# One accumulator for both parts of x, operands at multiples of 512 bytes, and moved steps in a hybrid decoder layer

## The chip, the cores and the metric

The kernel runs on one core of a Trainium2 chip. TensorE multiplies, VectorE, ScalarE and GpSimd work on elements, SyncE issues the transfers; each of them works through its own queue strictly in order. In the profile they are called PE (its weight loads PEld), DVE, ACT, POOL and SP. The metric is the device time of one execution in microseconds (us), the median of the runs; less is better.

## What is computed

One decoder layer on 256 tokens of width 1024, in float32. It has three parts, each followed by a residual and a layer norm:

```python
def swiglu(x, w_gate, w_up, w_down):
    return (jax.nn.silu(x @ w_gate) * (x @ w_up)) @ w_down
...
h = layer_norm(DEEPNORM_ALPHA * h + 0.5 * swiglu(h, ffn1_w_gate, ffn1_w_up, ffn1_w_down), ln1_g, ln1_b)
h = layer_norm(DEEPNORM_ALPHA * h + hybrid_mixer(h, w_in, ...), ln2_g, ln2_b)
h = layer_norm(DEEPNORM_ALPHA * h + 0.5 * swiglu(h, ffn2_w_gate, ffn2_w_up, ffn2_w_down), ln3_g, ln3_b)
```

Both SwiGLU blocks have 2816 inner columns. The mixer projects h with `w_in` into z, xBC (4096 columns), dt, q, k, v and two gates. xBC goes through a causal depthwise convolution of four taps and SiLU, then through a chunked scan (Mamba-2 SSD) of 8 groups; q, k and v go through causal attention of 8 heads; both branches are projected, gated, added and projected once more.

## The kernel before

**Products in three parts.** Every float32 operand is held as a pair of float32r tiles, hi (the rounded value) and lo (what is left). A product is hi·hi + lo·hi + hi·lo, accumulated in PSUM. `xT` holds x transposed, as [128, 8 k-tiles, 2 parts, 256 tokens], so the two parts of a k-tile lie side by side.

**The weight stream.** 126 weight tiles of 1 MB (2048 columns a partition) run through three buffers each of `raw`, `hi` and `lo`. A tile is prepared in two pieces of 1024 columns: ACT casts `hi<-raw` (line 91), and DVE, for some pieces POOL, subtracts `lo<-raw,hi` (line 100). `step()` moves a counter on by one before every batch of products; it runs what tables have due at this count, prepares the next pieces (hi four ahead, lo three ahead, or up to a number given as `upto`), and runs what was put behind them. `at`, `later`, `after` and `at_mid` fill these tables, so the order on each engine is written by hand. A step of a token-major product is 12 matmuls of 512 columns (`mm3`: four hi·hi, four lo·hi, then what is due "mid", then four hi·lo).

**Weights-stationary products** (`fmm`, `wstat`) have 128 weight columns standing still and x moving. For each of four k-tiles there is one matmul of 512 columns, both parts of x at once (line 274), and then one of 256 columns for lo of the weights (line 276). A call therefore makes 8 matmuls; the left half of the accumulator holds the sum for x hi, the right half that for x lo, and the product is their sum. In the kernel 240 such calls run: 72 in each SwiGLU, 64 for xBC, 32 for q and k. Who takes a product copies the right half with ACT into `fb` and adds the left half with DVE one step later: `gate` (line 392) and `h` (400) in SwiGLU, `pre` (598) ahead of the convolution, `qk` (148 is the line that runs tabled calls). The convolution of a 128-column block is then one ACT multiplication and three DVE multiply-adds on `pre` and `cv`, both in SBUF (line 608). PSUM has eight banks: four for `mmt` tiles, four for `smt` tiles.

**The order around the boundaries.** After the first SwiGLU come the layer norm, 16 steps of z, 32 of xBC, 16 of q and k. The decay `dt` goes through a long chain of small POOL and DVE operations, which ends in `da` (line 564); `acum_mm` (569 to 575) multiplies it by a triangular matrix in step 15 of the mixer, between two batches of z. The scan groups start after xBC and are spread over the steps of q, k, v and the gates. At the end of the mixer eight steps of the output projection `wo` run, four for the first 128 tokens, four for the others; after each half comes `ln`, and `to_T` transposes the normalised tokens again into `xT` (lines 242 to 246) in the middle of a later step. Then the second SwiGLU starts with `gu`, x standing still.

**Places in SBUF.** Constant tiles are laid out in the order in which they are made, each rounded up to 32 bytes. `tok`, `ident` and `tri` start 128 bytes past a multiple of 512, `xT` 192 bytes past one; the weight tiles, `hTh` and `hTl` start at multiples of 512.

Of the kernel before, what the change touches and what calls it, by code (L numbers as in the profile page):

```python
# [15 lines left out]
P = 128  # L16
# [23 lines left out]
def tile_decoder_layer(ctx: ExitStack, tc: tile.TileContext,  # L40
# [18 lines left out]
    # ---------------------------------------------------------------- weight stream  # L59
    # Every tile holds 2048 columns a partition, in two pieces of 1024: raw from DRAM, then hi + lo in float32r.  # L60
# [72 lines left out]
    def after(d, fn, *a):  # L133
        """As later, but behind the pieces of that step."""
        at_after(clk["n"] + d, fn, *a)

    def step(i, h, upto=None):
        """The next products, on tile i: what is due, then the pieces to come."""
# [3 lines left out]
        if upto is not None:  # L142
            stream(2 * i + upto, 2 * i + upto)
# [6 lines left out]
    def first_order(tiles, n=3):  # L150
        """Both token blocks of every tile; t = 1 of the first n tiles comes after their t = 0."""
# [21 lines left out]
    # ---------------------------------------------------------------- the order of the weights  # L173
# [34 lines left out]
    s_f2 = ffn_specs(f2g, f2u, f2d, [(), (1,), (0, 1), ()])  # L208

    # ---------------------------------------------------------------- constants and inputs  # L210
# [25 lines left out]
    xT = const.tile([P, KD, 2, S], F32R, name="xT")  # L236
# [23 lines left out]
    def xmm(ps, k0, t, i):  # L260
        """ps (tokens of t, 512) += x k-tiles k0.. times the weight tile i: x stands still."""
# [699 lines left out]
```

## Time and profile before

| | |
|---|---|
| median of 3 runs | 799.17 us (798.56 to 799.29) |
| span of the profiled execution | 794.7 us |
| time of a run beyond that span | about 4.5 us |
| PE, DVE, ACT, POOL busy | 97%, 70%, 55%, 18% |
| matmuls, and weight loads | 4042, and as many |
| moved by DMA | 143.61 MB, mean 181 GB/s |
| granted TensorE clock, mean | 0.990 |

The span goes from the first to the last instruction of the profiled execution. A run's time also holds what lies around it, so a sum made on the span has 4.5 us added before it is set beside the median. PE's busy time is modelled: a matmul is recorded with its full latency, and the next one starts before it has ended. What a matmul costs in a dense run is the distance between the starts of two of them, not its duration.

### The profile page before, as it was taken

How to read it: one execution, taken by the hardware profiler on the slowest of the kernel's cores; microseconds unless marked ns; L12 is line 12 of the kernel's file. 1: busy time of each engine (PE TensorE's matmuls, PEld its weight loads, DVE VectorE, ACT ScalarE, POOL GpSimd, SP SyncE). 2: the span in 40 equal slices, each digit the busy share in tenths (PEclk: the TensorE clock that was granted, in tenths of full speed). 3: DMA queues.
4: the chain of work that ended last, by engine and by line, in shares of the span. 5: the costliest groups of instructions: out<-in, count | busy, mean ns of one | idle time of the engine just before them, and what ended most of it. 6: DMA issues, size and time to landing. Idle time of an engine off the chain costs nothing.

```text
span 794.7 us, 10749 instructions
## 1 busy us (share of the span) xinstructions
PE 767.6 (97%) x4042; PEld 651.4 (82%) x4042; DVE 556.2 (70%) x817; ACT 438.7 (55%) x766; POOL 142.8 (18%) x217
## 2 busy tenths in 40 slices
PE   7999999999999999998999999999998999999996
PEld 6888888888777888777888878888887888888885
DVE  4676667448533999998877786776686677667446
ACT  5565556333554666678666663575553555656420
POOL 1000000004042222202866764000012000000000
PEclk9999999999998999999999999999999999999998
DMA  8666665673544454467555534444564576556611
GB/s 317 219 215 220 202 212 169 206 261 106 165 159 160 154 165 159 159 212 232 166 186 185 159 123 172 159 157 134 182 214 158 189 235 212 178 193 212 210 55 54
DMA packets 68356, 143.61 MB, mean 181 GB/s; under 512 B 3968, under 2 KB 8528, under 8 KB 68304
## 3 DMA queue, kind: packets, MB, share of 16 engines
q1 hardware_dynamic: 68160, 142.79, 54.1%
q8 instruction: 32, 0.52, 0.3%
q14 instruction: 20, 0.16, 0.1%
q10 hardware_dynamic: 144, 0.13, 0.0%
HBM read 141.83 MB, written 1.08 MB: 180 GB/s over the span
## 4 chain that ended last, share of the span: by engine, by line
PE 51%; DVE 14%; issue 5%; POOL 3%; ACT 3%; DVEq 0%; ACTq 0%; POOLq 0%
PE w L274 12%; PE w L276 6%; DVE cv L608 6%; DVE lo L100 5%; PE b L252 5%; PE b L258 5%; PE b L254 5%; PE dn L252 2%; PE dn L254 2%; PE dn L258 2%; PE yp L692 2%; ACT hi L91 1%; PE gu L254 1%; PE gu L258 1%; DVE pre L598 1%
## 5 line engine op out<-in xcount | busy, mean ns | idle before, releaser
L100 DVE TENSOR_TENSOR lo<-raw,hi 128x1024 fp32r<-128x1024 f32 x235 | 295.4, 1272 | 96.1 <-ACT hi L91 95.0
L91 ACT CAST hi<-raw 128x1024 fp32r<-128x1024 f32 x252 | 259.2, 1046 | 95.7 <-issue 37.6
L274 PE MATMUL w<-xT,hi 128*128 128x512 f32 x960 | 262.4, 396 | 4.4 <-DVE qk L148 3.0
L274 PEld LDWEIGHTS w<-xT,hi 128*128 128x128 f32 x960 | 163.2, 188 | 26.9 <-DVE qk L148 3.4
L276 PEld LDWEIGHTS w<-xT,lo 128*128 128x128 f32 x960 | 145.3, 188 | 25.4 <-DVE lo L100 4.2
L276 PE MATMUL w<-xT,lo 128*128 128x256 f32 x960 | 149.6, 278 | 3.3 <-DVE lo L100 3.2
L100 POOL TENSOR_TENSOR lo<-raw,hi 128x1024 fp32r<-128x1024 f32 x17 | 43.7, 2584 | 354.3 <-DVE lo L100 187.2
L608 DVE SCALAR_TENSOR_TENSOR cv<-pre,vecs,cv 128x255 f32<-128x255 f32 (+2 forms) x96 | 63.6, 666 | 2.4
L387 ACT COPY fb<-w 128x256 f32<-128x256 f32 x72 | 26.8, 373 | 54.5 <-PE w L276 53.6
L258 PE MATMUL dn<-lo,hTh 128*128 128x512 f32 (+1 forms) x176 | 47.9, 377 | 0.0
L254 PE MATMUL dn<-hi,hTl 128*128 128x512 f32 (+1 forms) x176 | 47.8, 377 | 0.0
L252 PE MATMUL dn<-hi,hTh 128*128 128x512 f32 (+1 forms) x176 | 47.8, 377 | 0.0
L254 PEld LDWEIGHTS dn<-hi,hTl 128*128 128x128 f32 x176 | 32.3, 188 | 6.2
L258 PEld LDWEIGHTS dn<-lo,hTh 128*128 128x128 f32 x176 | 32.2, 188 | 5.9
L252 PEld LDWEIGHTS dn<-hi,hTh 128*128 128x128 f32 x176 | 31.7, 188 | 5.7
L343 POOL TENSOR_TENSOR tok<-tok,lng 128x256 f32<-128x256 f32 x1 | 0.9, 872 | 187.9 <-ACT tok L340 187.9
L614 ACT ACTIVATE g<-cv 128x256 f32<-128x256 f32 x32 | 13.3, 416 | 33.5 <-DVE cv L608 33.1
L320 ACT ACTIVATE lnmv<-lnmv,epsc 128x1 f32<-128x1 f32 x6 | 1.8, 296 | 52.2 <-DVE lnmv L319 52.2
L252 PE MATMUL b<-hi,xT 128*128 128x512 f32 x96 | 27.6, 409 | 0.0
L258 PE MATMUL b<-lo,xT 128*128 128x512 f32 x96 | 25.9, 392 | 0.0
L254 PE MATMUL b<-hi,xT 128*128 128x512 f32 x96 | 25.8, 391 | 0.0
L254 PEld LDWEIGHTS b<-hi,xT 128*128 128x128 f32 x96 | 18.0, 188 | 4.0
(209 smaller groups left out, 1063.4 us busy)
## 6 DMA issues: line engine op xcount, KB each, us to landing
raw<-in_w_in_dram SPq DMA_DIRECT2D x44, 1024.0 KB, 5.0
raw<-in_ffn_w_up_dram SPq DMA_DIRECT2D x22, 1024.0 KB, 5.1
raw<-in_ffn_w_down_dram SPq DMA_DIRECT2D x22, 1024.0 KB, 4.8
raw<-in_ffn_w_gate_dram SPq DMA_DIRECT2D x21, 1024.0 KB, 5.0
raw<-in_w_ssm_out_dram SPq DMA_DIRECT2D x8, 1024.0 KB, 5.0
acb<-dsc SPq DMA_DIRECT2D x8, 512.0 KB, 3.8
raw<-in_w_att_out_dram SPq DMA_DIRECT2D x4, 1024.0 KB, 5.2
raw<-in_w_o_dram SPq DMA_DIRECT2D x4, 1024.0 KB, 4.9
```

The source lines that it names most:

```text
L91: A.copy(ready[i][0][:, s], raws[i][:, s])
L100: e.tensor_tensor(lo[:, s], raws[i][:, s], hi[:, s].bitcast(F32), op=ALU.subtract)
L252: T.matmul(ps, ah, bh, start=first, stop=False)
L254: T.matmul(ps, al, bh, start=False, stop=False)
L258: T.matmul(ps, ah, bl, start=False, stop=last)
L274: T.matmul(ps, hi[:, k, fs], xT[:, k0 + k].rearrange("p h s -> p (h s)"), start=k0 + k == 0, stop=False)
L276: T.matmul(ps[:, 0:S], lo[:, k, fs], xT[:, k0 + k, 0], start=False, stop=k0 + k == KD - 1)
L387: A.copy(b, ps[:, S:2 * S])
L598: V.tensor_tensor(pre, ps[:, 0:S], b, op=ALU.add)
L608: V.scalar_tensor_tensor(cv[:, m:], pre[:, :S - m], cw(3 - m, ft), cv[:, m:], op0=ALU.mult, op1=ALU.add)
L614: A.activation(dst, cv, AF.Silu)
L692: T.matmul(yp[:, o:o + 64], mt[:, c, h], xd[:, c, h], start=True, stop=True)
```

## The change

- `fmm` has two matmuls of 256 columns for each k-tile where it had one of 512: x hi, then x lo, with the same weights, into the same 256 columns of PSUM. A call has 12 matmuls of 256 columns; the accumulator is the product.
- The copies `fb` and the additions behind them are gone. In SwiGLU, `gate` is SiLU on ACT straight from PSUM, `h` is one DVE multiplication of PSUM and `gate`, and the split of `h` into `hTh` and `hTl` is done for two blocks at once. The convolution reads the accumulator in PSUM in its first multiplication and its three multiply-adds. `qk` is a DVE copy.
- `brow` (384 bytes) and `xT` are made before the other constants, so that `xT`, `tok`, `ident` and `tri` start at multiples of 512 bytes.
- `acum_mm` runs in step 19 of the mixer, which is in xBC, and no longer in step 15.
- At the boundary to the second SwiGLU, `ln` of the first tokens has its `to_T` three steps later and no longer four; the lo pieces prepared in the last four `wo` steps reach less far ahead; none of the second SwiGLU's lo pieces is on POOL.
- `ln` of the second tokens runs a one-column SiLU behind its square root, which brings the load of the activation table there.

```diff
         for k in range(nk):
-            T.matmul(ps, hi[:, k, fs], xT[:, k0 + k].rearrange("p h s -> p (h s)"), start=k0 + k == 0, stop=False)
+            T.matmul(ps, hi[:, k, fs], xT[:, k0 + k, 0], start=k0 + k == 0, stop=False)
+            T.matmul(ps, hi[:, k, fs], xT[:, k0 + k, 1], start=False, stop=False)
         for k in range(nk):
-            T.matmul(ps[:, 0:S], lo[:, k, fs], xT[:, k0 + k, 0], start=False, stop=k0 + k == KD - 1)
+            T.matmul(ps, lo[:, k, fs], xT[:, k0 + k, 0], start=False, stop=k0 + k == KD - 1)
...
-            def part(f, ps, fn):
-                b = fp.tile([P, S], F32, name="fb", tag="fb", bufs=4)
-                A.copy(b, ps[:, S:2 * S])
-                after(1, fn, f, ps, b)
...
-                V.tensor_tensor(gate[f], ps[:, 0:S], b, op=ALU.add)
-                after(1, gate2, f)
...
+                A.activation(gate[f], ps, AF.Silu)
...
-                V.tensor_tensor(h, ps[:, 0:S], b, op=ALU.add)
-                V.tensor_tensor(h, h, gate.pop(f), op=ALU.mult)
-                after(1, up2, f, h)
+                V.tensor_tensor(h[:, f % 2], ps, gate.pop(f), op=ALU.mult)
+                if f % 2:
+                    after(1, up2, f - 1, h)
...
-        later(15, acum_mm)
+        later(19, acum_mm)
...
         def conv(b, f, ps):
-            fb = ma.tile([P, S], F32, name="fb", tag="qk", bufs=18)
-            A.copy(fb, ps[:, S:2 * S])
-            after(1, conv_0, 4 * b + f, ps, fb, clk["n"] + 2 + f // 2 + f % 2)
+            at(clk["n"] + 1 + f // 2 + f % 2, conv_1, 4 * b + f, ps)
...
-            A.copy(b, ps[:, S:2 * S])
             t_ = ma.tile([P, S], F32, name=f"qk{len(qk)}", tag="qk", bufs=18)
             qk.append(t_)
-            after(1, V.tensor_tensor, t_, ps[:, 0:S], b, ALU.add)
+            after(1, V.tensor_copy, t_, ps)
...
-            step(s_wo[0][3], 0, upto=(3, 5, 7, 7, 8, 10, 12, 13)[q])
+            step(s_wo[0][3], 0, upto=(3, 5, 7, 7, (9, 8), (11, 9), (12, 10), (13, 11))[q])
...
-                    ln(t, 3 + (t == 0), 3 + (t == 0))
+                    ln(t, 3, 3)
```

On DVE, at the first blocks of the convolution, there is before (`pre` is the sum in SBUF, `cv` the result, `w` the accumulator):

```order
L598 TENSOR_TENSOR pre<-w_2074,fb 128x256
L598 TENSOR_TENSOR pre<-w_2075,fb 128x256
L608 SCALAR_TENSOR_TENSOR cv<-pre,vecs,cv 128x255
L608 SCALAR_TENSOR_TENSOR cv<-pre,vecs,cv 128x254
L608 SCALAR_TENSOR_TENSOR cv<-pre,vecs,cv 128x253
L100 TENSOR_TENSOR lo_2206<-raw_2095,hi_2174 128x1024
```

And on DVE in the same place now:

```order
L100 TENSOR_TENSOR lo_2252<-raw_2158,hi_2222 128x1024
L600 SCALAR_TENSOR_TENSOR cv<-w_2218,vecs,cv 128x255
L600 SCALAR_TENSOR_TENSOR cv<-w_2218,vecs,cv 128x254
L600 SCALAR_TENSOR_TENSOR cv<-w_2218,vecs,cv 128x253
L100 TENSOR_TENSOR lo_2318<-raw_2192,hi_2286 128x1024
```

The addition `pre` has gone from the queue, and the three multiply-adds have one operand in PSUM.

On PE, around the product with the triangular matrix, there is before, between two token halves of z:

```order
L258 MATMUL z_1_2009<-lo_1891,xT 128x512 x4
L569 MATMUL acum<-da,tri 128x64
L571 MATMUL acum<-tri,da 32x128 x2
L252 MATMUL z_0_1991<-hi_1925,xT 128x512 x4
L254 MATMUL z_0_1991<-hi_1925,xT 128x512 x4
```

And on PE now, behind the first half of the first block of xBC:

```order
L278 MATMUL w_2221<-xT,lo_2161 128x256 x4
L565 MATMUL acum<-da,tri 128x64
L567 MATMUL acum<-tri,da 32x128 x2
L275 MATMUL w_2218<-xT,hi_2176 128x256
L276 MATMUL w_2218<-xT,hi_2176 128x256
```

The six small matmuls stand four steps later, behind the rest of z and two steps of xBC.

On DVE, at the boundary to the second SwiGLU, from the end of the first tokens' `ln` to the transposed x, there is before:

```order
L329 SCALAR_TENSOR_TENSOR tok<-tok,lnmv,lnb 128x512
L100 TENSOR_TENSOR lo_5375<-raw_5308,hi_5373 128x1024 x2
L100 TENSOR_TENSOR lo_5393<-raw_5328,hi_5390 128x1024
L313 SCALAR_TENSOR_TENSOR tok<-wo_5285,tok 128x512
L314 BN_STATS lnst<-tok 128x6
L246 TENSOR_TENSOR xT<-xt_190_5441,xT 128x4x128
L246 TENSOR_TENSOR xT<-xt_190_5448,xT 128x4x128
```

And on DVE now:

```order
L333 SCALAR_TENSOR_TENSOR tok<-tok,lnmv,lnb 128x512
L100 TENSOR_TENSOR lo_5762<-raw_5694,hi_5759 128x1024 x2
L100 TENSOR_TENSOR lo_5796<-raw_5714,hi_5776 128x1024
L248 TENSOR_TENSOR xT<-xt_189_5806,xT 128x4x128
L248 TENSOR_TENSOR xT<-xt_189_5813,xT 128x4x128
L315 SCALAR_TENSOR_TENSOR tok<-wo_5671,tok 128x512
L316 BN_STATS lnst<-tok 128x6
```

The lo part of the transposed x stands ahead of the residual of the second tokens. Of the three lo pieces that POOL had in this stretch, DVE now has one between the two residuals of the second tokens and two behind their `ln`.

## Rows read from the trace of the kernel before

**Rows 1.** Page, part 1: busy us (share of span) and instructions by engine.

```profile
PE 767.6 (97%) x4042; PEld 651.4 (82%) x4042; DVE 556.2 (70%) x817; ACT 438.7 (55%) x766; POOL 142.8 (18%) x217
```

**Rows 2.** Timeline, PE, first SwiGLU: start us, us, engine, line, what, count.

```profile
71.61 1.09 PE L274 MATMUL w<-xT,hi 128*128 128x512 f32 x4
72.54 0.62 PE L276 MATMUL w<-xT,lo 128*128 128x256 f32 x4
...
77.16 1.09 PE L274 MATMUL w<-xT,hi 128*128 128x512 f32 x4
```

**Rows 3.** Timeline, PE, the last down projection: runs of 512, then of 256 columns.

```profile
778.34 0.62 PE L252 MATMUL dn<-hi,hTh 128*128 128x512 f32 x2
...
780.61 0.62 PE L258 MATMUL dn<-lo,hTh 128*128 128x512 f32 x2
...
781.77 0.40 PE L252 MATMUL dnx<-hi,hTh 128*128 128x256 f32 x2
...
786.57 0.40 PE L258 MATMUL dn<-lo,hTh 128*128 128x256 f32 x2
```

**Rows 4.** Timeline, PE, down projection: two trios of 512, 256 and 256 columns.

```profile
729.52 0.40 PE L254 MATMUL dn<-hi,hTl 128*128 128x512 f32 x1
...
730.47 0.40 PE L258 MATMUL dn<-lo,hTh 128*128 128x512 f32 x1
```

**Rows 5.** Timeline around `acum`; windows row (us, PE, PEld, DVE, ACT, POOL, PEclk, DMA, GB/s).

```profile
236.43 1.08 PE L258 MATMUL z<-lo,xT 128*128 128x512 f32 x4
...
240.23 0.66 PE L569 MATMUL acum<-da,tri 128*128 128x64 f32 x2 [2.72 <-DVE da L564]
...
246.81 1.09 PE L252 MATMUL z<-hi,xT 128*128 128x512 f32 x4
...
239.60:246.50 6.90, 6.27 (x17) 4.76 (x18) 3.35 (x6) 2.41 (x3) 0.14 (x1) 0.51 0.20 43
```

**Rows 6.** DVE's groups from 249.5 to 345.5 us, and line 608's durations (min/median/max).

```profile
L608 DVE SCALAR_TENSOR_TENSOR cv<-pre,vecs,cv 128x255 f32<-128x255 f32 (+2 forms) x79 | 54.6, 695 | 1.9
L100 DVE TENSOR_TENSOR lo<-raw,hi 128x1024 fp32r<-128x1024 f32 x21 | 25.6, 1221 | 7.2 <-ACT hi L91 6.8
L598 DVE TENSOR_TENSOR pre<-w,fb 128x256 f32<-128x256 f32 x28 | 10.7, 418 | 4.6 <-ACT fb L618 4.6
...
L608 DVE SCALAR_TENSOR_TENSOR cv<-pre,vecs,cv x96: 472/482/2702, 261.8 to 361.7; 128x255 f32<-128x255 f32 x32, 128x254 f32<-128x254 f32 x32, 128x253 f32<-128x253 f32 x32
```

**Rows 7.** Timeline, PE: first product of xBC, first of q and k, two waits.

```profile
249.57 1.10 PE L274 MATMUL w<-xT,hi 128*128 128x512 f32 x4
...
343.88 1.09 PE L274 MATMUL w<-xT,hi 128*128 128x512 f32 x4
...
348.08 1.20 PE L274 MATMUL w<-xT,hi 128*128 128x512 f32 x4 [1.01 <-DVE pre L598]
...
360.48 1.19 PE L274 MATMUL w<-xT,hi 128*128 128x512 f32 x4 [2.79 <-DVE qk L148]
```

**Rows 8.** Timeline, the boundary to the second SwiGLU.

```profile
591.64 7.90 DVE L100 TENSOR_TENSOR lo<-raw,hi 128x1024 fp32r<-128x1024 f32 x3
...
592.47 9.28 POOL L100 TENSOR_TENSOR lo<-raw,hi 128x1024 fp32r<-128x1024 f32 x3 [95.53 <-ACT hi L91]
...
598.19 1.08 PE L252 MATMUL gu<-hi,xT 128*128 128x512 f32 x4
...
599.46 0.68 DVE L313 SCALAR_TENSOR_TENSOR tok<-wo,tok 128x512 f32<-128x512 f32 x1
...
601.51 2.07 PE L254 MATMUL gu<-hi,xT 128*128 128x512 f32 x4 [2.24 <-DVE xT L246]
...
604.99 1.08 PE L252 MATMUL gu<-hi,xT 128*128 128x512 f32 x4
```

**Rows 9.** Timeline, PE, the boundary from the first SwiGLU to z.

```profile
203.71 1.20 PE L252 MATMUL z<-hi,xT 128*128 128x512 f32 x4 [0.79 <-ACT xT L245]
```

**Rows 10.** Timeline, PE, a scan group: sixteen matmuls of 64 columns.

```profile
369.82 1.89 PE L692 MATMUL yp<-xd,dec 128*128 128x64 f32 x16
```

More of the change, by code (lines that the diff above doesn't have):

```diff
@@ L142, in step @@
         if upto is not None:
-            stream(2 * i + upto, 2 * i + upto)
+            u, v = upto if isinstance(upto, tuple) else (upto, upto)
+            stream(2 * i + u, 2 * i + v)
         else:
@@ L207, in tile_decoder_layer @@
             for k0 in (0, 4) for j in range(2)]
-    s_f2 = ffn_specs(f2g, f2u, f2d, [(), (1,), (0, 1), ()])
+    s_f2 = ffn_specs(f2g, f2u, f2d, [()] * 4)
+    brow = const.tile([P, 3, HEADS], F32, name="brow")
+    xT = const.tile([P, KD, 2, S], F32R, name="xT")
     tok = const.tile([P, 2, D], F32, name="tok")
@@ L234, in tile_decoder_layer @@
     G.memset(epsc, EPS_LN)
-    xT = const.tile([P, KD, 2, S], F32R, name="xT")
     def to_T(t, j):
@@ L286, in wstat @@
             return
-        ps = [smt(f"w{clk['n']}{f}") if both and f > 1 else mmt(f"w{clk['n']}{f}") for f in range(4)]
+        ps = [(smt if both and f > 1 else mmt)(f"w{clk['n']}{f}")[:, 0:S] for f in range(4)]
         for kh in range(2):
@@ L320, in ln @@
         A.activation(mv[:, 2:3], mv[:, 1:2], AF.Sqrt, bias=epsc, scale=1.0)
+        if t and not last:
+            A.activation(junk, epsc, AF.Silu)
         V.reciprocal(mv[:, 3:4], mv[:, 2:3])
@@ L383, in ffn, with gate1, up1 @@
             gate = {}
-            def part(f, ps, fn):
-                b = fp.tile([P, S], F32, name="fb", tag="fb", bufs=4)
-                A.copy(b, ps[:, S:2 * S])
-                after(1, fn, f, ps, b)
-            def gate1(f, ps, b):
-                gate[f] = fp.tile([P, S], F32, name="gate", tag="gate", bufs=6)
-                V.tensor_tensor(gate[f], ps[:, 0:S], b, op=ALU.add)
-                after(1, gate2, f)
-            def gate2(f):
-                A.activation(gate[f], gate[f], AF.Silu)
-            def up1(f, ps, b):
-                h = fp.tile([P, S], F32, name="h", tag="h", bufs=4)
-                V.tensor_tensor(h, ps[:, 0:S], b, op=ALU.add)
-                V.tensor_tensor(h, h, gate.pop(f), op=ALU.mult)
-                after(1, up2, f, h)
+            def gate1(f, ps):
+                gate[f] = fp.tile([P, S], F32, name="gate", tag="gate", bufs=6)
+                A.activation(gate[f], ps, AF.Silu)
+            def up1(f, ps):
+                if f % 2 == 0:
+                    gate["h"] = fp.tile([P, 2, S], F32, name="h", tag="h", bufs=2)
+                h = gate["h"]
+                V.tensor_tensor(h[:, f % 2], ps, gate.pop(f), op=ALU.mult)
+                if f % 2:
+                    after(1, up2, f - 1, h)
             def up2(f, h):
-                A.copy(hTh[:, f], h)
+                A.copy(hTh[:, f:f + 2], h)
                 after(1, up3, f, h)
             def up3(f, h):
-                V.tensor_tensor(hTl[:, f], h, hTh[:, f].bitcast(F32), op=ALU.subtract)
+                V.tensor_tensor(hTl[:, f:f + 2], h, hTh[:, f:f + 2].bitcast(F32), op=ALU.subtract)
             for f0, gt, ut in [(4 + 4 * b, *mid[b]) for b in range(NB)] + [(FL, last[:1], last[1:])]:
-                wstat(gt, lambda f, ps: part(f0 + f, ps, gate1))
-                wstat(ut, lambda f, ps: part(f0 + f, ps, up1))
+                wstat(gt, lambda f, ps: after(1, gate1, f0 + f, ps))
+                wstat(ut, lambda f, ps: after(1, up1, f0 + f, ps))
             after(3, A.activation, junk, epsc, AF.Sqrt)
@@ L467, in tile_decoder_layer @@
     vecs = const.tile([P, 192], F32, name="vecs")
-    brow = const.tile([P, 3, HEADS], F32, name="brow")
     def vec_load():
@@ L595, in tile_decoder_layer @@
         grp = [mp.tile([P, 4, S], F32, name=f"g{g}", tag="g4", bufs=9) for g in range(GROUPS)]
-        def conv_0(ft, ps, b, taps):
-            pre = ma.tile([P, S], F32, name="pre", tag="qk", bufs=18)
-            V.tensor_tensor(pre, ps[:, 0:S], b, op=ALU.add)
-            at(taps, conv_1, ft, pre)
         def conv_1(ft, pre):
@@ L774, in qk_out @@
         def qk_out(f, ps):
-            if f % 2 == 0:
-                wk["fb"] = mp.tile([P, 2, S], F32, name="fb", tag="bg")
-            b = wk["fb"][:, f % 2]
-            A.copy(b, ps[:, S:2 * S])
             t_ = ma.tile([P, S], F32, name=f"qk{len(qk)}", tag="qk", bufs=18)
             qk.append(t_)
-            after(1, V.tensor_tensor, t_, ps[:, 0:S], b, ALU.add)
+            after(1, V.tensor_copy, t_, ps)
         for b in range(4):
```

2 lines of the change are left out of this document (1 added, 1 removed).

## The prediction, made before the changed kernel was run

> **What bounds the kernel now.** I read the page's busy line first: PE is busy for 97% of the span [rows 1], but with recorded latencies that overlap, so the line says only that PE is where to look. The timeline of PE says more. In the SwiGLU stages the weights-stationary calls follow each other without a gap, one call of four 512-column and four 256-column matmuls every (77.16 - 71.61) / 4 = 1.388 us [rows 2]. There nothing but the cost of a matmul counts; whatever DVE and ACT save is hidden. From the first convolution until the first scan groups it is otherwise. From 249.5 to 345.5 us DVE's three groups alone hold 54.6 + 25.6 + 10.7 = 90.9 of 96 us, and PE waits for it: xBC takes 343.88 - 249.57 = 94.3 us where its 64 calls need 64 x 1.388 = 88.8, and the start of q and k waits twice more [rows 6, 7]. Then three boundaries have stalls of their own [rows 5, 8, 9]. So the kernel is a PE-bound stream with about 20 us of holes, and the change makes the stream denser in instructions and closes holes. The sum is made on the profiled execution: span 794.7 us, and 4.5 us around it to the median of 799.17.
>
> **The change part by part.**
>
> *Two matmuls for one.* This is the dearest question. A call goes from 4 x 512 + 4 x 256 columns to 12 x 256, the same 3072 columns in 12 matmuls with 12 weight loads instead of 8. The trace has no long run of such calls, but it has runs of 256 columns with a new weight load each. At the end of the program they start (786.57 - 781.77) / 40 = 0.120 us apart; just ahead, 512-column ones start (780.61 - 778.34) / 10 = 0.227 apart [rows 3]. Two of 256 thus cost 0.240 for 0.227. A call at 0.120 takes 1.440 us, 0.052 more than now, and 240 calls 12.6 us. The bound below: within a present call the four 256-column matmuls take what is left of the period, 1.388 - (72.54 - 71.61) = 0.458 us, 0.114 each [rows 2]; all twelve at that pace are 1.374 us, 0.014 less than now, and 240 calls give 3.4 us back. The bound above: a trio of one 512 and two 256 takes (730.47 - 729.52) / 2 = 0.475 us [rows 4]; less 0.227, its two 256 take 0.248, so 0.124 each, 1.488 a call, 24.1 us in all. I take 0.120, because it is the one row with a long, unbroken run of 256 columns, with operands at multiples of 512 bytes on both sides, which is what the changed calls will be. In the present calls the short ones come in fours behind long ones, and x is not at such a multiple. +12.6.
>
> *xBC.* DVE loses the additions `pre`, 10.7 us in the window. The multiply-adds gain more: undisturbed they take 0.48 us, but the mean is 0.695, and the longest takes 2.70 [rows 6]. The long ones fall in POOL's subtractions (line 100), and they have two operands in SBUF. One with an operand in PSUM took 0.68 us for 512 columns in the middle of POOL's three subtractions at the second boundary [rows 8], no longer than DVE's pace elsewhere. So at most 0.48 each, 79 x 0.48 = 38 us, and DVE's demand falls from 91 to 64 of 96 us. PE then waits for nothing, and the 94.3 - 88.8 = 5.5 us of holes go. Against it stands that the accumulator is held until the last tap, up to three steps after its products; its bank comes up again two blocks, eight steps, later, so four steps remain. -5.5.
>
> *The start of q and k* waits 1.01 us for `pre` and 2.79 us for the additions of `qk`, both late because DVE is still behind from the convolution [rows 7]. The waits go with the backlog; the copies from PSUM that replace the additions stand in the same place of the queue. -3.8.
>
> *acum.* PE stands 2.72 us ahead of line 569 for `da`, and in that stretch its granted clock is 0.51, so on the lower of its levels, 1.2 GHz; z goes at half pace for one step and more [rows 5]. From 236.43 four batches of four matmuls would bring z to where it is at 246.81; at z's pace of (249.57 - 246.81) / 12 = 0.230 us [rows 5, 7] they take 3.7 us, the six small matmuls some 0.7 at the full clock (an estimate from 0.118 each [rows 10]), and 10.4 - 4.4 = 6.0 us are lost. Four steps later `da` has long been there: z has two steps to go after it, then xBC has two. What is queued behind the moved product on ACT and DVE are the next pieces, four and three ahead, which the wait for PE does not use up. The gap goes, and with it the low clock, as PE was not idle ahead of it. -6.0.
>
> *The second SwiGLU's start.* From 598.19 to 604.99 PE does 12 matmuls, 2.8 us at z's pace; 4.0 are lost, by a wait of 2.24 us for the lo part of x and a low clock behind it [rows 8]. The lo part comes late since DVE's subtractions ahead of it take 7.90 us for three while POOL subtracts [rows 8] (1.22 each elsewhere [rows 6]), and a residual is queued ahead of it. Now POOL has none, and the transposed x goes ahead of the residual, a whole step earlier. Next comes the subtraction of the third tile, two pieces behind the second tokens' norm on DVE: laid on the old times they end about 0.4 us after PE asks for them. -3.6.
>
> *The first boundary* has 0.79 us for ACT's cast of x [rows 9], which is queued behind a SiLU and the load of its table; the table is now loaded while ACT is idle. -0.8.
>
> *Alignment.* With x standing still at an odd place, z starts a matmul every 0.230 us; the down projection, all at multiples of 512, every 0.227 [rows 3, 5, 7]. If place makes the difference, the 672 such matmuls in z, v, the gates and both `gu` gain 0.003 us each. -2.0. From below zero it is bounded by the same rows the other way, +2.0, should the new place be worse. The Trainium skill, page "SBUF — State Buffer", section "Who interferes with whom", has two independent read ports for PE and names no engine that it waits for; by that the term is nothing and the sum 792.1, and the rows that differ speak against it.
>
> *Hidden.* In SwiGLU the copies `fb`, the additions and the split by twos all lie beside the matmuls: nothing. Should PE become faster there, DVE at 70% of the span [rows 1] leaves room. In the rest of the scan and in attention nothing changes but alignment.
>
> Sum: 12.6 - 5.5 - 3.8 - 6.0 - 3.6 - 0.8 - 2.0 = -9.1, a span of 785.6 and a time of **790.1 us**.
>
> **The rivals.**
>
> *The fast pace.* All twelve matmuls run at 0.114 us, as the fours do now. Then the first term is -3.4, and the time 774.1. For it: sixteen matmuls of 64 columns with a weight load each fit into 1.89 us [rows 10], at most 0.118 each, so neither loads nor issue need 0.120; and x will be aligned as it is not now. Against it: the aligned run in rows 3 does not reach it. The Trainium skill, "TensorE: Matmul & The Clock Gate", section "Back-to-back issue gap", goes further the same way: N columns every N / 2.4 + 2.5 ns, 109 and 216 ns. Neither row 3 pace agrees with it; by that difference of 2.6 ns a pair the first term would be 2.5 and the time 780.0.
>
> *Slower: the weight loads come too thick.* In a run of nothing but 256 columns, weights and x are read twice as often side by side as in a run of 512. If a matmul then costs 0.124, as in the trios, the first term is 24.1 and the time 801.6. It turns slower than before when the term passes 12.6 + 9.1 = 21.7, so at (1.388 + 0.0904) / 12 = 0.1232 us a matmul. For it: the trios [rows 4], and that the trace's longest run of 256 is 5 us, while this is most of 300. Against it: that run keeps its 0.120 from near its start to its end.
>
> *The holes move.* The holes in xBC, at q and k and at the second boundary come back elsewhere, because an accumulator is held too long or a lo piece is late; with most of these 12.9 us gone the time is about 800, no change. Against it: DVE's demand of 64 in 96 us.
>
> **How the numbers follow.** I give the forecast 0.62, the fast pace 0.20, the slow pace 0.10, the moved holes 0.08. The forecast's own range is 784 to 797: 0.001 us on a matmul is 2.9 us, and the holes may come out by 3 either way. The range for 8 in 10 takes in most of the fast pace and stops ahead of the slow one: 772 to 799. Within 0.2% is about what a measurement of this kernel can tell from no change, 797.6 to 800.8. Faster: the forecast, the fast pace and some of the moved holes, 0.83; the same 0.06; slower 0.11.
>
> **What would show it.** In the profile after: a call's period in SwiGLU, 1.44 us (1.37 for the fast pace, 1.49 for the slow one), and 5002 or so matmuls; xBC in 92 to 93 us with no wait of PE for lo or for an accumulator; DVE's multiply-adds near 0.45 us, none above 1; no wait at `acum` and a clock that stays high there and at the second boundary; z at 0.227 us a matmul. The forecast is wrong if the period is not near 1.44, or if PE shows waits in xBC of more than 2 us in all.

## The result and the profile after

The changed kernel takes 786.37 us, the median of four runs (785.86 to 788.28); the runs of before taken with it have a median of 798.87 (795.60 to 799.29). The ratio of the two, estimated from all of these runs, is 0.9859, with a 95% interval of 0.9836 to 0.9881 (the medians alone give 0.984). The forecast was 790.1 with a range of 772 to 799. The profiled execution has a span of 784.0 us and took 785.86.

The page of after, part 1 (busy us, share of the span, instructions), beside [rows 1]: PE has 960 matmuls more, and DVE 60 us less to do. Under it, from the list of PE's waits (waiter, whom for: us in all, times, longest), everything that is left:

```profile
PE 771.2 (98%) x5002; PEld 702.3 (90%) x5002; DVE 496.1 (63%) x698; ACT 400.1 (51%) x630; POOL 132.7 (17%) x214
```

```profile
PE gu L254 <- ACT hi L91: 1.9, 2, 1.2
PE warm L456 <- POOL ident L225: 1.4, 1, 1.4
PE yt L741 <- DVE ya L733: 1.1, 1, 1.1
PE sp L677 <- POOL xl L671: 0.6, 1, 0.6
```

None of the waits of [rows 5, 7, 8, 9] is in it. The timeline of PE shows the two things the sum rests on: the period of a call, and the places where the holes were. First a call of the first SwiGLU (L278 is its last four products), answering to [rows 2]; then the last products of z, the first of xBC and the first of q and k, answering to [rows 5, 7]:

```profile
71.66 0.64 PE L278 MATMUL w<-xT,lo 128*128 128x256 f32 x4
...
73.10 0.64 PE L278 MATMUL w<-xT,lo 128*128 128x256 f32 x4
```

```profile
240.64 1.07 PE L260 MATMUL z<-lo,xT 128*128 128x512 f32 x4
...
243.36 1.07 PE L260 MATMUL z<-lo,xT 128*128 128x512 f32 x4
244.26 0.28 PE L275 MATMUL w<-xT,hi 128*128 128x256 f32 x1
...
337.32 0.28 PE L275 MATMUL w<-xT,hi 128*128 128x256 f32 x1
```

The period is 73.10 - 71.66 = 1.44 us, 0.120 a matmul. z runs through at (243.36 - 240.64) / 12 = 0.227 a matmul. xBC takes 337.32 - 244.26 = 93.06 us; 64 x 1.44 are 92.16, and 0.8 of the rest is `acum`, which now lies in it.

The stretch in which [rows 5] had a granted clock of 0.51, and the one in which `acum` now lies, as rows of the windows view (columns as in [rows 5]): PE is at its upper level, 2.4 GHz, in both.

```profile
239.60:246.50 6.90, 6.90 (x41) 6.08 (x40) 4.84 (x5) 3.58 (x5) 4.72 (x2) 1.00 0.35 105
249.00:252.00 3.00, 3.00 (x26) 2.73 (x26) 0.80 (x3) 0.80 (x2) 0.00 (x0) 1.00 0.57 222
```

DVE's groups from 244 to 337.2 us and line 600's durations (min/median/max), answering to [rows 6]: the additions are gone, and no multiply-add is longer than 0.486 us, whatever POOL does beside it (28 of the 96 lie wholly inside one of POOL's subtractions).

```profile
L600 DVE SCALAR_TENSOR_TENSOR cv<-w,vecs,cv 128x255 f32<-128x255 f32 (+2 forms) x89 | 42.4, 480 | 8.8 <-ACT cv L595 6.7
L100 DVE TENSOR_TENSOR lo<-raw,hi 128x1024 fp32r<-128x1024 f32 x24 | 30.7, 1280 | 10.6 <-ACT hi L91 10.6
```

```profile
L600 DVE SCALAR_TENSOR_TENSOR cv<-w,vecs,cv x96: 469/481/486, 253.2 to 342.9; 128x255 f32<-128x255 f32 x32, 128x254 f32<-128x254 f32 x32, 128x253 f32<-128x253 f32 x32
```

The start of the second SwiGLU, answering to [rows 8]: DVE's three subtractions take 3.49 us in place of 7.90, and `gu` runs on without a wait.

```profile
581.45 3.49 DVE L100 TENSOR_TENSOR lo<-raw,hi 128x1024 fp32r<-128x1024 f32 x3
...
588.00 1.07 PE L254 MATMUL gu<-hi,xT 128*128 128x512 f32 x4
```

So much for the signs that the prediction asked for. Where the time went is read best from the starts of each stage's first product. The table does that for before, after, and two of the experiments below; all entries are us of a profiled execution.

| stage (from its first product to the next stage's) | before | after | b_bounds | a_mis |
|---|---|---|---|---|
| ahead of the first product | 6.57 | 6.88 | 7.13 | 6.87 |
| first SwiGLU, x standing still | 25.42 | 24.23 | 26.28 | 25.48 |
| first SwiGLU, 72 calls | 100.63 | 104.39 | 100.63 | 102.31 |
| z (and dt, `acum`) | 56.13 | 47.96 | 48.33 | 48.29 |
| xBC, 64 calls | 94.31 | 93.05 | 95.44 | 88.19 |
| q and k, first scan groups | 61.81 | 58.29 | 62.52 | 56.19 |
| v to the output projection | 192.51 | 192.39 | 192.49 | 192.61 |
| second SwiGLU, x standing still | 27.28 | 23.05 | 23.23 | 23.22 |
| second SwiGLU, 72 calls | 100.38 | 104.17 | 100.38 | 102.20 |
| both down projections and the end | 129.70 | 129.58 | 129.70 | 129.66 |
| from the first call to the end | 762.75 | 752.88 | 752.72 | 742.67 |

Where two kernels have the same code, products and places in a stage, that stage repeats within some 0.1 us from profile to profile; the long one from v to the output projection spreads over 0.3 (the other exceptions stand under the two rhythms below). The second row does not: over the eleven decoder profiles of this study it takes 24.2 to 28.0 us. So medians of like kernels can lie 2 to 3 us apart, and the last line of the table leaves the start out. Of the 12.5 us between the two medians, 762.75 - 752.88 = 9.87 lie behind the first call. The other 2.6 us are the start: an estimate, each span less what lies behind the first call, leaves 34.3 us for it in the four runs of before and 31.7 in those of after. The runs show no cause for that in the change: mix, whose start has the same code, gets 32.8 to 34.3 by the same estimate.

### The profile page after: what moved, and what is told of

Same layout as the page of the kernel before. It is cut to its first block, busy times and chain, and to the rows that moved or that the text cites. A ratio compares the mean times of both kernels' runs of the same rounds, so it can differ in the third digit from the quotient of the medians.

```text
span 784.0 us, 12362 instructions
## 1 busy us (share of the span) xinstructions
PE 771.2 (98%) x5002; PEld 702.3 (90%) x5002; DVE 496.1 (63%) x698; ACT 400.1 (51%) x630; POOL 132.7 (17%) x214
## 4 chain that ended last, share of the span: by engine, by line
PE 95%; DVE 2%; POOL 2%; issue 0%; ACT 0%; DVEq 0%; POOLq 0%
PE w L275 15%; PE w L278 15%; PE w L276 15%; PE dn L254 5%; PE dn L256 5%; PE dn L260 5%; PE b L254 5%; PE b L260 5%; PE b L256 5%; PE z L254 2%; PE z L256 2%; PE gu L260 2%; PE gu L256 2%; PE z L260 2%; PE gu L254 2%; PE yp L682 2%
## 5 line engine op out<-in xcount | busy, mean ns | idle before, releaser
L275 PE MATMUL w<-xT,hi 128*128 128x256 f32 x960 | 241.3, 284 | 0.0
L276 PE MATMUL w<-xT,hi 128*128 128x256 f32 x960 | 240.2, 283 | 0.0
L275 PEld LDWEIGHTS w<-xT,hi 128*128 128x128 f32 x960 | 184.1, 192 | 0.2 <-issue 0.2
L276 PEld LDWEIGHTS w<-xT,hi 128*128 128x128 f32 x960 | 184.2, 192 | 0.0
L278 PE MATMUL w<-xT,lo 128*128 128x256 f32 x960 | 153.0, 283 | 0.0
L278 PEld LDWEIGHTS w<-xT,lo 128*128 128x128 f32 x960 | 131.9, 192 | 0.0
L100 POOL TENSOR_TENSOR lo<-raw,hi 128x1024 fp32r<-128x1024 f32 x14 | 35.5, 2546 | 247.0 <-DVE lo L100 190.1
L600 DVE SCALAR_TENSOR_TENSOR cv<-w,vecs,cv 128x255 f32<-128x255 f32 (+2 forms) x96 | 45.8, 480 | 8.9 <-ACT cv L595 6.7
L254 PEld LDWEIGHTS dn<-hi,hTh 128*128 128x128 f32 x176 | 31.7, 188 | 5.7
L397 DVE TENSOR_TENSOR h<-w,gate 128x256 f32<-128x256 f32 x36 | 15.2, 422 | 19.3 <-PE w L278 19.3
L260 PE MATMUL b<-lo,xT 128*128 128x512 f32 x96 | 25.7, 390 | 0.0
```

Of the source, the lines that this page charges most:

```text
L100: e.tensor_tensor(lo[:, s], raws[i][:, s], hi[:, s].bitcast(F32), op=ALU.subtract)
L254: T.matmul(ps, ah, bh, start=first, stop=False)
L260: T.matmul(ps, ah, bl, start=False, stop=last)
L275: T.matmul(ps, hi[:, k, fs], xT[:, k0 + k, 0], start=k0 + k == 0, stop=False)
L276: T.matmul(ps, hi[:, k, fs], xT[:, k0 + k, 1], start=False, stop=False)
L278: T.matmul(ps, lo[:, k, fs], xT[:, k0 + k, 0], start=False, stop=k0 + k == KD - 1)
```

## The experiments

### The boundaries alone: b_bounds

```
-        later(15, acum_mm)
+        later(19, acum_mm)
...
-    s_f2 = ffn_specs(f2g, f2u, f2d, [(), (1,), (0, 1), ()])
+    s_f2 = ffn_specs(f2g, f2u, f2d, [()] * 4)
...
-            step(s_wo[0][3], 0, upto=(3, 5, 7, 7, 8, 10, 12, 13)[q])
+            step(s_wo[0][3], 0, upto=(3, 5, 7, 7, (9, 8), (11, 9), (12, 10), (13, 11))[q])
...
-                    ln(t, 3 + (t == 0), 3 + (t == 0))
+                    ln(t, 3, 3)
```

with the early load of the SiLU table, as in the change.

> Before, with only the reordered boundaries: acum four steps later, the order of weight pieces and x at the start of the second SwiGLU, no lo pieces on POOL there, and the SiLU table loaded early. Calls of 512 and 256 columns, the copies and additions and the places are as before. Theory (the holes are those of single places and go with their cause): acum 6.0, second SwiGLU 3.6, first boundary 0.8, so 10.4 less: 788; no wait ahead of acum, and a granted clock of 1.0 there. Rival (z or xBC gets a new hole of the same length when acum comes later): 794 or more.

Measured: 787.49 us, ratio 0.9889 (0.9854 to 0.9923). z shortens by 7.8 us and the second start by 4.05. Of the 7.8, 0.8 is `acum`, which only moved into xBC; xBC and the stage of q and k get 1.1 and 0.7 longer. From the first call to the end that is 762.75 - 752.72 = 10.0 us, for 10.4 expected. The holes that the products were to close are all still there; here two of them, and DVE's queue in xBC, in the same views as in [rows 6, 7]:

```profile
342.81 1.20 PE L275 MATMUL w<-xT,hi 128*128 128x512 f32 x4 [1.00 <-DVE pre L601]
...
355.04 1.22 PE L275 MATMUL w<-xT,hi 128*128 128x512 f32 x2 [2.64 <-DVE qk L149]
```

```profile
L611 DVE SCALAR_TENSOR_TENSOR cv<-pre,vecs,cv 128x255 f32<-128x255 f32 (+2 forms) x78 | 53.7, 692 | 2.6 <-ACT cv L606 0.7
```

The last line of the table holds the finding of the study: b_bounds and after are equal, 752.72 and 752.88. **The whole gain of the change comes from its boundaries.** Its products and its places together add nothing to that: they close the holes of xBC and of q and k and pay for it in the SwiGLU stages. The next runs take the two apart.

### The places alone: b_align and a_mis

b_align is before with brow and xT allocated first; a_mis is after with both where before had them:

```
-    brow = const.tile([P, 3, HEADS], F32, name="brow")
-    xT = const.tile([P, KD, 2, S], F32R, name="xT")
     tok = const.tile([P, 2, D], F32, name="tok")
...
     G.memset(epsc, EPS_LN)
+    xT = const.tile([P, KD, 2, S], F32R, name="xT")
...
     vecs = const.tile([P, 192], F32, name="vecs")
+    brow = const.tile([P, 3, HEADS], F32, name="brow")
```

> Before, with nothing changed but the places: brow and xT are allocated first, so x, the tokens and the identity lie at multiples of 512 bytes. Theory: z, v, gates and gu go from 0.230 to 0.2275 a matmul, 2.0 us, and the 512s inside the 240 calls, 0.232 on the mean, go to 0.227: 960 x 0.005 = 4.8 if the short ones stay at 0.115, so 792 to 797 in all. Rival (place does nothing; the pace of z in after came with the denser stream): 799, z at 0.230. Rival (the whole gain of after is the place): 786.

Measured: 798.35 us, ratio 1.0015 (0.9996 to 1.0033), and no theory as it stands: z's stage gets 1.43 us shorter, but the two SwiGLU stages get 2.00 us longer, since the calls got longer. From the timeline of the first SwiGLU:

```profile
71.74 1.09 PE L274 MATMUL w<-xT,hi 128*128 128x512 f32 x4
...
73.14 1.09 PE L274 MATMUL w<-xT,hi 128*128 128x512 f32 x4
```

A call takes 1.40 us where it took 1.388 [rows 2]; the matmuls alone, below, show the same.

> After, with nothing changed but the places: brow and xT are allocated where they were before, x at 192 bytes past a multiple of 512. Theory: z and the others go back to 0.230, +2.0, and the twelve 256s of a call, being short of column time by the same share, cost up to 0.003 more each, 2880 x 0.003 = 8.6: 788 to 797. Rival (short matmuls run at 0.113 with x off a multiple, as in the calls of before): 2880 x 0.006 = 17 less, 771. Rival (place does nothing): 786.

Measured: 775.95 us, ratio 0.9713 (0.9677 to 0.9749), and 774.05, ratio 0.9723 (0.9698 to 0.9747), when it ran again as a_mis_5. My theory had the sign wrong: **with x where it lay before, the kernel is some 10 us faster** than with x at a multiple of 512 bytes. Set against b_bounds, which has the same places, a_mis shows what the products give by themselves: 752.72 - 742.67 = 10.05 us (13.6 in a_mis_5). The new places take as much away. The last four products of two calls in xBC, and of two in the first SwiGLU:

```profile
300.20 0.62 PE L278 MATMUL w<-xT,lo 128*128 128x256 f32 x4
301.56 0.62 PE L278 MATMUL w<-xT,lo 128*128 128x256 f32 x4
```

```profile
72.00 0.64 PE L278 MATMUL w<-xT,lo 128*128 128x256 f32 x4
73.42 0.63 PE L278 MATMUL w<-xT,lo 128*128 128x256 f32 x4
```

A call takes 1.36 us in xBC, 0.1133 a matmul, and 1.42 in SwiGLU (1.413 over many calls), 0.118. What the multiple of 512 gives to the products with x standing still is small: z, v to the output projection, and the second start are 0.33 + 0.22 + 0.17 = 0.7 us longer in a_mis, and the 0.22 is within that stage's spread.

### The pace by itself: pace and pace2

pace holds nothing but matmuls. The edit is the kernel; one of its runs is

```
    for k in range(128):
        T.matmul(a256[:, 0:256], ws(k % 16, 0), xs(k % 16, 256, 0), start=k == 0, stop=k == 127)
```

and the others change the columns and the two offsets, in elements of four bytes.

> Not the decoder layer: only runs of 128 fp32r matmuls with a weight load each, nothing beside them on the other engines, with the moving operand or the weights at a multiple of 512 bytes or 192 bytes past one; then sixteen calls in the pattern of before (four of 512 columns, four of 256) and sixteen in the pattern of after (twelve of 256), each with x at either place. Theory of the prediction (a matmul of 256 with its weight load costs 0.120 by itself, a matmul of 512 0.227 at a multiple and 0.230 off it): aligned 256 starts every 0.120 us, aligned 512 every 0.227, the call of after takes 1.44, the call of before 1.39. Rival 1 (0.120 is what the other engines' work beside it costs): here 256 takes 0.113 or less and the call of after 1.36. Rival 2 (the 0.113 of the short matmuls of before comes from x lying off a multiple): 256 with x at 192 takes 0.113 and at 0 takes 0.120. Rival 3 (it comes from the long ones ahead of them): every unbroken run of 256 takes 0.120 wherever x lies, and the call of before is 1.39 at both places.

The timeline of PE, in order: 256 columns with both operands at a multiple of 512 bytes; x 192 bytes past it; the weights past it; both past it; then 512 columns with both at it, x past it, the weights past it; and 256 with x 64, then 256 bytes past it.

```profile
22.18 15.52 PE L69 MATMUL a<-xa,wa 128*128 128x256 f32 x128
37.53 14.69 PE L73 MATMUL b256x<-xa,wa 128*128 128x256 f32 x128
52.06 14.67 PE L77 MATMUL c256w<-xa,wa 128*128 128x256 f32 x128
66.56 15.52 PE L81 MATMUL d256both<-xa,wa 128*128 128x256 f32 x128
81.92 29.22 PE L85 MATMUL e<-xa,wa 128*128 128x512 f32 x128
110.98 30.03 PE L89 MATMUL f512x<-xa,wa 128*128 128x512 f32 x128
140.84 30.03 PE L93 MATMUL g512w<-xa,wa 128*128 128x512 f32 x128
170.71 15.24 PE L97 MATMUL h256x<-xa,wa 128*128 128x256 f32 x128
185.79 15.51 PE L101 MATMUL i256x<-xa,wa 128*128 128x256 f32 x128
```

From one start to the next, over 128: 0.1199, 0.1135, 0.1133, 0.1200 for 256 columns; 0.2270, 0.2333, 0.2333 for 512; 0.118 for x 64 bytes off. The last row, which ends at 201.13 where the next run starts, has 0.120 again. It is not the multiple that counts but the place of x against that of the weights: both moved give 0.120 again. Off by 192 bytes, the short ones gain 0.0066 us and the long ones lose 0.0063. No engine works beside them, so rival 1 falls; unbroken runs differ by place, so rival 3 falls; rival 2 stands. The two patterns of a call bear it out (the twelve of 256 with x at 192; then the call of before, first aligned, then with x at 192):

```profile
325.90 0.62 PE L139 MATMUL o_pairx<-xa,wa 128*128 128x256 f32 x4
327.26 0.62 PE L139 MATMUL o_pairx<-xa,wa 128*128 128x256 f32 x4
```

```profile
252.20 1.09 PE L114 MATMUL l_call<-xa,wa 128*128 128x512 f32 x4
...
253.60 1.09 PE L114 MATMUL l_call<-xa,wa 128*128 128x512 f32 x4
...
266.22 1.09 PE L121 MATMUL m_callx<-xa,wa 128*128 128x512 f32 x4
...
267.61 1.09 PE L121 MATMUL m_callx<-xa,wa 128*128 128x512 f32 x4
```

Twelve short ones take 1.36 us at 192, and 1.44 aligned (in the same run, 305.30 to 306.74). The call of before takes 1.387 at 192 and 1.403 aligned, as in b_align: in that pattern the long ones take 0.232 on the mean at either place, and the fours of short ones 0.1146 at 192 and 0.1185 aligned. So a call's pace need not be the sum of what unbroken runs of each length give, which aligned would be 1.388. And the change's two ideas work against each other: it makes every product short, and moves x to the place where short products are slowest. The Trainium skill, page "SBUF — State Buffer", section "Who interferes with whom", gives PE two read ports that are independent and says that PE never waits on anyone; these rows, with only PE at work, show a pace that depends on where its own two operands lie against each other, by 6% at 256 columns and 3% at 512, and the measurement decides.

> Not the decoder layer: only matmuls. The weights lie at multiples of 512 bytes, x lies 0, 32, 64, 96, 128, 160, 192, 224, 320, 384 or 448 bytes past one. For each place there are 8 matmuls of 128 columns, then 96 of 256, then 32 of 512, then 48 of 256, so that each run of 256 starts once behind short ones and once behind long ones. What was seen before this run: 0.120 a matmul of 256 at 0, 0.118 at 64, 0.1135 at 192; and in the decoder layer with x at 192 the same call took 1.413 in SwiGLU (0.118 a matmul) and 1.360 (0.113) in xBC. Theory of place alone: each place has one pace whatever ran ahead, mirrored about 256 (64 as 448, 192 as 320). Theory of two rhythms: at 192 both 0.113 and 0.118 can last, and which of them depends on what ran ahead, so that the two runs of 256 at one place differ at some place.

Here x lies at eleven places. The runs of 96 and of 48 matmuls agree at every place, so this run shows one pace for each, and nothing of two rhythms. Two of the places, 0 and 192:

```profile
22.51 11.73 PE L70 MATMUL o<-xa,wa 128*128 128x256 f32 x96
34.08 7.45 PE L72 MATMUL o<-xa,wa 128*128 128x512 f32 x32
...
174.66 11.12 PE L130 MATMUL o<-xa,wa 128*128 128x256 f32 x96
185.62 7.62 PE L132 MATMUL o<-xa,wa 128*128 128x512 f32 x32
```

Over 96 that is 0.1205 and 0.114, the entry included. 192 and 448 are alike (0.114), and so are 64 and 320 (0.118): the pace repeats every 256 bytes, and is not mirrored as I had thought. Of the eleven, none is faster for short products than 192 and 448.

### The convolution from a copy in SBUF: a_convsb

```
-            at(clk["n"] + 1 + f // 2 + f % 2, conv_1, 4 * b + f, ps)
+            pre = ma.tile([P, S], F32, name="pre", tag="qk", bufs=18)
+            A.copy(pre, ps)
+            at(clk["n"] + 1 + f // 2 + f % 2, conv_1, 4 * b + f, pre)
```

> After, with one copy more: ACT copies each product of xBC from PSUM to SBUF and the convolution reads that, as it did before, but with no addition on DVE. Theory (a multiply-add with both operands in SBUF stands while POOL subtracts): multiply-adds of over 1 us come back wherever POOL subtracts, their mean goes from 0.48 to 0.6 or 0.7, and DVE has 10 to 18 us more to do in xBC; PE may wait 0 to 3 us: 786 to 790. Rival (the long ones came with the additions, or from DVE's queue being late): no multiply-add over 0.6 us, and the same time as after, 786.

Measured: 789.25 us, ratio 0.9903 (0.9873 to 0.9933). DVE's group of multiply-adds in xBC, their durations (min/median/max), and from the timeline the start of q and k:

```profile
L600 DVE SCALAR_TENSOR_TENSOR cv<-pre,vecs,cv 128x255 f32<-128x255 f32 (+2 forms) x81 | 55.7, 693 | 6.3 <-ACT cv L595 4.0
```

```profile
L600 DVE SCALAR_TENSOR_TENSOR cv<-pre,vecs,cv x96: 471/482/2702, 256.7 to 351.4; 128x255 f32<-128x255 f32 x32, 128x254 f32<-128x254 f32 x32, 128x253 f32<-128x253 f32 x32
```

```profile
353.45 0.36 PE L275 MATMUL w<-xT,hi 128*128 128x256 f32 x1 [1.64 <-DVE qk L149]
```

The mean of 693 ns and the longest of 2702 are those of [rows 6], with no addition on DVE. All nine that take over 0.6 us overlap a subtraction of POOL; two rows of the timeline show one such place, where six multiply-adds take 4.97 us in place of 2.9:

```profile
263.41 4.97 DVE L600 SCALAR_TENSOR_TENSOR cv<-pre,vecs,cv 128x255 f32<-128x255 f32 x6
264.12 2.55 POOL L100 TENSOR_TENSOR lo<-raw,hi 128x1024 fp32r<-128x1024 f32 x1 [7.05 <-ACT hi L91]
```

So it is the operand in SBUF that makes a multiply-add stand while POOL subtracts, and reading PSUM that frees it. The Trainium skill, in the same section of "SBUF — State Buffer", says that an instruction of DVE with two inputs in SBUF contends with one of GpSimd that reads SBUF; 693 ns against 480 agrees. xBC stays at 93.05 us, so here DVE's lag costs PE nothing until q and k start, where 1.64 us come back.

### Long products where the copies are hidden: mix and mix192

mix gives the SwiGLU calls of after the products, copies and additions of before:

```
-                wstat(gt, lambda f, ps: after(1, gate1, f0 + f, ps))
-                wstat(ut, lambda f, ps: after(1, up1, f0 + f, ps))
+                wstat(gt, lambda f, ps: part(f0 + f, ps, gate1), wide=True)
+                wstat(ut, lambda f, ps: part(f0 + f, ps, up1), wide=True)
```

> After, but the 144 calls of both SwiGLU stages again as before: four products of 512 columns and four of 256, the copy of x's lo half by ACT and the addition by DVE. xBC, q and k stay at twelve of 256. Theory (the copies and additions are hidden in SwiGLU, the denser products cost 0.052 a call everywhere): 144 x 0.052 = 7.5 less than after, 779. If x at a multiple also takes the 512s of a call from 0.232 to 0.227, 144 x 4 x 0.005 = 2.9 more, 776. Rival (the copies and additions cost PE waits in SwiGLU that after has shed): 786 or more.

Measured: 782.74 us, ratio 0.9813 (0.9787 to 0.9838). The two SwiGLU stages take 101.71 and 101.30 us: 5.6 less than in after, and not 7.5, since the aligned call takes 1.40 and not 1.387, as in b_align. The copies and additions are hidden: PE waits for none of them.

> The run mix (SwiGLU with products of 512 and 256 columns, copies and additions; xBC, q and k with twelve of 256), with x at 192 bytes past a multiple of 512. Theory (for each place and pattern the pace of the matmul-only runs or of before holds): SwiGLU calls take 1.387 as before and not 1.403, xBC 1.360 and not 1.440: 144 x 0.016 + 96 x 0.080 = 10.0 less than mix, less 1.4 that z, v, the gates and gu lose: 774. Rival (the gain of a_mis came with the twelve-matmul calls of SwiGLU alone): 780 or more.

Measured: 774.39 us, ratio 0.9694 (0.9672 to 0.9716). The SwiGLU stages are back at 100.63 and 100.38, to 0.01 us those of before, and xBC takes 88.00. This is the step from mix that was expected, 8.6 us from the first call to the end (747.56 to 738.99) for 8.6 worked out (10.0 less 1.4).

### The two rhythms: kick192 and a second look at a_mis

kick192 is a_mis with one product of 512 columns ahead of the ninth call of each SwiGLU:

```
+                if kick and kh + h == 0:
+                    T.matmul(wide, wt(tiles[0])[0][:, 0, 0:P], xT[:, 0].rearrange("p h s -> p (h s)"), start=True, stop=True)
```

> After with x at 192 bytes past a multiple of 512 (the run a_mis), and in each SwiGLU one matmul of 512 columns ahead of the ninth call, into the bank that this call then starts anew; its product is not used. In a_mis, 65 and 70 calls from the seventh and the third call on went at 1.413 us in SwiGLU, those of xBC at 1.360. Theory of two rhythms (what ran just ahead decides which one lasts; behind 512 columns the matmul-only run went straight into 0.113): the calls behind the extra product take 1.360, 134 x 0.053 = 7.1 less, 2 x 0.23 more, 776 - 6.7 = 769. Rival (in SwiGLU it is the work of the other engines that makes 1.413): 1.413 comes back within a call or two, 776.5.

Measured: 774.57 us, ratio 0.9697 (0.9664 to 0.9729), and in the profile what the theory says. The extra product (L295) and the last four products of the two calls behind it:

```profile
44.38 0.39 PE L295 MATMUL w<-xT,hi 128*128 128x512 f32 x1
...
45.54 0.62 PE L278 MATMUL w<-xT,lo 128*128 128x256 f32 x4
...
46.90 0.62 PE L278 MATMUL w<-xT,lo 128*128 128x256 f32 x4
```

A call takes 46.90 - 45.54 = 1.36 us, and both SwiGLU stages 99.1 us in place of 102.3. The median, though, is 1.4 us below that of a_mis and not 6.7. So both ran again:

> The run a_mis again, beside kick192_5 on the same chip and in more rounds, for the difference of the two times: in the profiles they lie 6.2 us apart (spans of 775.0 and 768.8), in the medians 1.4. Theory (the rhythm of a call is the same in every execution): 775 to 776, and in the profile again 1.413 in SwiGLU and 1.360 in xBC. Rival (the rhythm falls by chance in each execution): the profile has other stretches at 1.413 than in a_mis, and the times spread over 768 to 777.

> The run kick192 again. Theory: 6 to 7 us less than a_mis_5, 769 to 770, and 1.360 from the ninth call on in both SwiGLU stages. Rival (the extra product decides only sometimes): within 3 us of a_mis_5, and one SwiGLU stage or both at 1.413 in the profile.

Measured: 774.05 us for a_mis_5, and 774.43, ratio 0.9731 (0.9708 to 0.9754), for kick192_5. In the profile of a_mis_5 the same program has another rhythm than before: from the eighth call of the first SwiGLU on,

```profile
71.74 0.62 PE L278 MATMUL w<-xT,lo 128*128 128x256 f32 x4
73.10 0.62 PE L278 MATMUL w<-xT,lo 128*128 128x256 f32 x4
```

1.36 us a call, while the second SwiGLU stays at 1.413. So the rhythm is not fixed by the program, and my theory for a_mis_5 fell. a_mis and a_mis_5 ran on two chips, but kick192 and kick192_5 ran on one, and they differ too: the first three calls of xBC take 1.413 us in the one and 1.36 to 1.38 in the other. In the timelines the rhythm changes only where other products (transposes, `acum`, the extra one) or a gap come between two calls, and then lasts. Of the four SwiGLU stages profiled without the extra product one was fast; of the four with it, all. From the first call to the end that is 742.67 and 739.09 without, 736.30 and 736.21 with. But the medians of the two kernels do not differ, and the start ahead of the first call, 25.4 to 28.0 us in these four profiles, spreads too little to hide 3 to 6 us. No profile has more than 34.9 us ahead of the first call; with 736.3 behind it a span would be at most 771.2 us (an estimate), and the eight executions of kick192 and kick192_5 that were not profiled have spans of 771.6 to 774.7. So the extra product probably did not hold in most of them, and its four out of four is in part luck. What in PE makes the two rhythms stays open.

Three versions thus beat both kernels by about the same: a_mis, mix192 and kick192, at 774 to 776 us, 3% below before and 10 to 12 us below after.

## Why the prediction was right, step by step

- **Two matmuls for one, +12.6.** Right: the period is 1.440 us, the SwiGLU stages are 3.76 and 3.79 us longer, for 72 x 0.052 = 3.74 each. The value was taken from the right rows (the aligned run of [rows 3]), but for a reason that I held only half: I had put it down to the run being long and unbroken as much as to the place. pace has unbroken runs of 256 columns at 0.120 and at 0.113, and only the place differs. Where I named x's coming alignment as a point *for* the fast pace of 0.114, it was the point against it; and the short products of [rows 2] went at 0.114 mostly because x was off: behind long ones, pace has 0.1146 with x off and 0.1185 with x aligned.
- **xBC, -5.5.** Right: 93.05 us for 92 to 93, no wait for lo or for an accumulator, and multiply-adds at 0.48. DVE's demand is 42.4 + 30.7 = 73.1 of 93 us and not 64, since more of the pieces fall into the stage (24 for 21, and 1.28 us each for 1.22). That is probably because DVE no longer lags: a_convsb, where PE is not held up in xBC either but DVE lags, has 21 again. a_convsb shows the reason given for the long multiply-adds, both operands in SBUF beside POOL. It also shows that the 5.5 us did not hang on them: with the long ones back and 55.7 + 25.7 = 81.4 us of demand, xBC takes the same 93.05 us without a wait. That the additions went was enough; the faster multiply-adds pay only where q and k start.
- **The start of q and k, -3.8.** The direction was right, the size too small: the stage is 3.52 us shorter though its 32 calls cost 1.7 more, so 5.2 us of holes went. a_convsb, where a wait of 1.64 is left, has 1.88 more than after, so a wait costs some 15% more than its idle time. That brings 3.8 to 4.4. The trace of before has two small waits more here that the prediction left out, 0.17 us for `qk` and 0.2 of a weight load for a lo piece; some 0.4 is not assigned.
- **acum, -6.0, and the first boundary, -0.8.** Right: with 0.7 for the six small products, which went to xBC, and 0.6 for the place of x, 8.1 were laid on z; it is 8.17 shorter. b_bounds has 7.8 without the new place.
- **The second start, -3.6.** Right: 4.05 in b_bounds; 4.23 in after with the new place.
- **Alignment, -2.0.** Mis-sized: after against a_mis gives 0.7 us for 576 of the 672 products, 0.0012 each and not 0.003. In dense runs, from before to after, z goes from 0.2298 to 0.2274 us a matmul, near the rows that were read, but v and the gates only from 0.2293 to 0.2285: the rows of z were taken for all.
- **The first SwiGLU's start** was forecast at no change beyond that, and is 1.2 us shorter. The other profiles show this to be the spread of the start.
- **The time around the span, 4.5 us.** This is the step that was furthest off: 2.7 of the 3.7 us between 790.1 and 786.37. I set the span of one execution of before, 794.7, against the median of all. In the later runs the span of every single execution is known, and each time lies 1.7 to 1.9 us above its own (796.6 in 798.37, 784.0 in 785.86); the spans of before run from 792.3 to 797.7. So the 4.5 held 1.8 around a span and 2.7 by which the profiled execution of before was ahead of the median. With 1.8 in place of 4.5 the sum gives 787.4.

The span came out at 784.0 for 785.6. From the first call to the end 9.87 us went, for 8.8 of the 9.1 forecast (the other 0.3 was alignment in the first start). That this is so near is in part luck: q and k gave 1.4 us more than the sum has for them, and alignment in v and the gates 0.8 less.

The rivals: the fast pace and the slow pace did not come, since 0.120 held from the first call to the last; the holes did not move, but for 0.7 us at q and k in b_bounds, where the multiply-adds still stand behind POOL. The Trainium skill's formula for an isolated matmul, page "TensorE: Matmul & The Clock Gate", section "Back-to-back issue gap", gives 109 ns for 256 columns (an estimate; two of 256 then cost 2.5 ns more than one of 512, not the 2.6 of the prediction). No run of 256 columns reaches it here: 113.3 ns at the best place.

What the prediction did not see is that its largest term was a choice of the change and not a price of short products: left at its old place, x would have made that term 240 x (1.360 - 1.388), a gain, wherever the fast rhythm holds. And no part of it said that products and places together come to nothing, though its own terms do (12.6 - 5.5 - 3.8 - 2.0 = 1.3; measured 752.88 - 752.72 = 0.2).

## What to carry to other kernels

Where PE is the bound, look at how far apart matmuls of each length start, in the trace and in a small kernel of matmuls alone with the operands at several distances from each other, before choosing the length of a product or moving a tile: the place of one operand against the other was worth 6% of a matmul of 256 columns here and 3% of one of 512, with opposite sign, and a mix of both lengths had a pace of its own. Do the parts of a change one by one, since a gain in one (the boundaries, 10 us) can hide that two others undo each other. And add a sum of stages to the span it was read from, never to a median of other executions.

## What the runs showed of the hardware that was not expected

- With one pair of places and one program, twelve matmuls of 256 columns have two paces that each last for 60 calls and more, 1.360 and 1.413 us a call, and which of them comes can differ between two executions (a_mis and a_mis_5; kick192 and kick192_5 on one chip). With both operands at a multiple of 512 bytes every run here settles at 1.440.
- In pace, a run of 64 columns with a weight load each starts at 0.112 us a matmul and ends at 0.213: the granted clock is 1.00 in the run of 128 columns ahead of it, 0.84 on the mean of 216 to 222 us, in which it falls from one level to the other, and 0.50, the lower level of 1.2 GHz, in the second part, though PE is never idle. Later, in the calls behind it, it is 1.00 again (windows view, columns as in [rows 5]):

```profile
201.00:215.00 14.00, 14.00 (x128) 14.00 (x127) 0.23 (x1) 0.00 (x0) 0.00 (x0) 1.00 0.00 1
216.00:222.00 6.00, 6.00 (x48) 6.00 (x47) 0.00 (x0) 0.00 (x0) 0.00 (x0) 0.84 0.01 3
224.00:238.00 14.00, 14.00 (x68) 14.00 (x67) 0.00 (x0) 0.00 (x0) 0.00 (x0) 0.50 0.00 0
247.00:262.00 15.00, 15.00 (x87) 13.10 (x87) 0.00 (x0) 0.00 (x0) 0.00 (x0) 1.00 0.00 1
```
